# Issuing the FFN input projections in the order of the text

## The chip, the cores and the metric
The kernel runs on one core of a Trainium2 chip. The metric is the device time of one execution in microseconds (us). The engines are TensorE (PE; its weight loads are listed as PEld), VectorE (DVE), ScalarE (ACT), GpSimd (POOL) and SyncE (SP), which here only issues loads.

## The reference, cut to what matters
One step of a two-layer encoder for two request groups, 1024 new frames and 64 frames of a running stream, in float32. Each layer has a mixer and then a gated FFN with a causal convolution of width 3:

```python
def conv_ffn(h, st, w_in, conv_w, conv_b, w_out):     # h: rmsnorm(x), width 1024; D_FF = 2816
    gu = h @ w_in
    g, u = gu[..., :D_FF], gu[..., D_FF:]
    g, new_st = causal_dwconv(g, conv_w, conv_b, st)
    return (jax.nn.gelu(g) * u) @ w_out, new_st
```

The change concerns `h @ w_in` in both layers, and the convolution and gelu beside it.

## The kernel before, in words
Tokens lie along the free dimension (1092 columns with four of padding), channels along the partitions. Float32 accuracy comes from splitting each operand into a rounded part `h` and a remainder `l` and adding three products (`wh x h`, `wl x h`, `wh x l`).

`ffn` (L867) goes through 22 groups for each layer. A group makes two output tiles of 128 channels; a *gate* group makes two tiles of g, and the *up* group after it the two of u that belong to them. A gate and an up group are called a pair here: 11 pairs a layer. For each group `seven` (L396) computes two token blocks of 428 columns with seven products of a half-depth matrix scheme (W, Z1, X1, X2, Z2, X3, Y; 12 instructions of 128x428 each, "wide") and the third block of 236 columns in the plain way (V1 and V0, 24 instructions of 128x236 each, "narrow"): 132 matmul instructions. The results lie in two PSUM tiles of three parts, one bank each: `ta` holds pw, v1, v0, and `tb` holds px, py, pz (L398 to L400). There are two buffers for them, so the next group's tile needs the former one to be read out.

- `held` (L410, tile `cp`) copies a part to SBUF on ScalarE: w, p5, p1, u2. X2 adds onto px after p1 is copied, X3 after u2 is, and Z2 adds onto pz after p5 is.
- `put` (L882 in a gate group, L903 in an up group) adds a part and a copy on VectorE.
- `plain` (L895 gate, L910 up) reads v1 or v0 on VectorE; the one of an up group multiplies by the gelu's result.
- `end` does the rest: for a gate group a multiplication by the norm (L887), the convolution (first tap L248 on ScalarE, two taps L250 on VectorE for each tile), gelu (L890) and another multiplication (L891); for an up group a multiplication (L906) and the store to DRAM (L907, issued by POOL).

The weights of a group are four pairs (h, l) of `ring` tiles: a2, a1, s24, s31. There are eight ring buffers, all in use, so a new pair takes the place of the former group's pair of that name once its last product has read it (V1 for a2, Y for a1, Z2 for s24, X3 for s31). `Ready` (L348) loads two raw tiles through SP (L357; two buffers) and makes one pair with each `step()`: ScalarE rounds (L373), VectorE subtracts (L374), and for a2 and a1 VectorE also makes two combinations in the raw tile (L378, L379; L383, L384).

The order of the work: the framework's planner lists each engine's instructions by priority (the place in the text) and by when it reckons their inputs to be there; it may bring a later instruction forward. It also sets all waits, from which tile an instruction reads or writes. Each engine then runs its list strictly in order. In the text of a middle group the products stand as W, V1, Z1, X1, V0, X2, Y, Z2, X3.

Of the kernel before, what the change touches and what calls it, by code (L numbers as in the profile page):

```python
# [10 lines left out]
AF = mybir.ActivationFunctionType  # L11
# [7 lines left out]
PAD = 4  # L19
S0 = L + PAD  # L20
T = S0 + LS
# [3 lines left out]
SB = 428  # L25
# [5 lines left out]
CONVS = {"ssd": (12, 4), "sc": (8, 3), "lru": (8, 4), "ffn0": (FT, 3), "ffn1": (FT, 3)}  # L31
# [23 lines left out]


def program(nc, tc, a, ctx):
    V, S, G, TE = nc.vector, nc.scalar, nc.gpsimd, nc.tensor
    const = ctx.enter_context(tc.tile_pool(name="const", bufs=1))
    sl = ctx.enter_context(tc.tile_pool(name="sl", bufs=1))  # L60
    wp = ctx.enter_context(tc.tile_pool(name="wp", bufs=1))
# [27 lines left out]
    def wk(cols=T):  # L89
        return slot("wk", 5, F, cols)  # L90
# [8 lines left out]
    def psum():  # L99
        n_of["pm"] = n_of.get("pm", 0) + 1  # L100
        return pm.tile([P, NB, 512], F, tag="pm", name=f"pm{n_of['pm']}")
# [19 lines left out]
    def col(key, i=0, n=1, rows=P):  # L121
        return par[0:rows, AT[key] + i:AT[key] + i + n]
# [33 lines left out]
    def step():  # L156
        if between:
            try:
                next(between[0])
            except StopIteration:  # L160
                between.pop(0)
# [77 lines left out]
        G.memset(cb[:, 0:PAD], 0.0)  # L239
        G.tensor_copy(cb[:, PAD + S0 - n:PAD + S0], col(kind + "_h", i * n, n))  # L240

    def conv(cb, kind, i, out):
        w = CONVS[kind][1]
        history(cb, kind, i)
        G.tensor_copy(keep[kind][:, i, 0], cb[:, PAD + L - w + 1:PAD + L])
        G.tensor_copy(keep[kind][:, i, 1], cb[:, PAD + T - w + 1:PAD + T])
        at = PAD - w + 1
        S.activation(out, cb[:, at:at + T], AF.Identity, bias=col(kind + "_b", i), scale=col(kind + "_w", i * w))  # L248
        for k in range(1, w):
            V.scalar_tensor_tensor(out, cb[:, at + k:at + k + T], col(kind + "_w", i * w + k), out, op0=OP.mult, op1=OP.add)  # L250

    def softplus(x, tmp1, tmp2):

# [15 lines left out]
    class Next:  # L269


        order = range(KT)
        ss = None

        def __init__(self, XR, key, spill=None):
            self.XR, self.key, self.xs, self.spill = XR, key, [], spill
# [18 lines left out]
        def rs(self):  # L295
            return rms(self.ss[0], D, self.ss[1])
# [96 lines left out]
            ready(*last[1])  # L393
            yield

    def seven(ws, X, put, plain, end, nxt, mode="mid", rs=None):  # L396

        ta, tb = psum(), psum()  # L398
        pw, v1, v0 = ta[:, 0, 0:SB], ta[:, 1, 0:RB], ta[:, 2, 0:RB]
        px, py, pz = tb[:, 0, 0:SB], tb[:, 1, 0:SB], tb[:, 2, 0:SB]  # L400

        def mul(ps, w, half, name, start=True, ks=range(HK)):
            for k in ks:
                at = slice((half * HK + k) * P, (half * HK + k + 1) * P)
                wh, wl = ws.w[w][0][:, at], ws.w[w][1][:, at]
                xh, xl = X.part(name, k)
                for i, (wx, x) in enumerate(((wh, xh), (wl, xh), (wh, xl))):
                    TE.matmul(ps, wx, x, start=start and k == 0 and i == 0, stop=k == HK - 1 and i == 2, skip_group_check=True)  # L408

        def held(ps):  # L410
            n = n_of["cp"] = n_of.get("cp", 0) + 1
            t = wp.tile([P, 512], F, tag="wh", bufs=4, name=f"cp{n}")[:, 0:SB]
            S.activation(t, ps, AF.Copy)  # L413
            return t

        def V1():
            mul(v1, "a2", 0, "k0")
            mul(v1, "a2", 1, "k1", False)

        def V0():  # L420
            mul(v0, "a1", 0, "k0")
            mul(v0, "a1", 1, "k1", False)

        def W():
            mul(pw, "a2", 1, "t4")

        def Z1():
            mul(pz, "s31", 1, "t1")

        def Z2():  # L430
            mul(pz, "s24", 1, "b22", False)

        def X1():
            mul(px, "a1", 0, "b11")

        def X2():
            mul(px, "s24", 0, "t2", False)

        def X3():
            mul(px, "s31", 0, "t3", False)  # L440

        def Y():
            mul(py, "a1", 1, "b21")

        step = nxt.step if nxt is not None else lambda: None
        if mode == "mid":
            W()
            V1()
            w = held(pw)
            Z1()  # L450
            plain(1, v1)
            step()
            X1()
            p5 = held(pz)
            V0()
            p1 = held(px)
            X2()
            Y()
            plain(0, v0)
            u2 = held(px)  # L460
            step()
            put(0, 0, py, p1)
            Z2()
        elif mode == "first":
            ws.step()
            Y()
            mul(v1, "a2", 1, "k1")
            mul(v0, "a1", 1, "k1")
            ws.step()
            for k in range(HK):  # L470
                mul(px, "a1", 0, "b11", True, [k])
                mul(pz, "s31", 1, "t1", True, [k])
                mul(pw, "a2", 1, "t4", True, [k])
                mul(v1, "a2", 0, "k0", False, [k])
                mul(v0, "a1", 0, "k0", False, [k])
            p1 = held(px)
            p5 = held(pz)
            w = held(pw)
            rs()
            plain(1, v1)  # L480
            step()
            X2()
            plain(0, v0)
            u2 = held(px)
            put(0, 0, py, p1)
            step()
            Z2()
        else:
            Z1()
            X1()  # L490
            p5 = held(pz)
            W()
            p1 = held(px)
            X2()
            w = held(pw)
            V1()
            u2 = held(px)
            V0()
            plain(1, v1)
            Y()  # L500
            plain(0, v0)
            put(0, 0, py, p1)
            Z2()
        step()
        X3()
        put(0, 1, pz, u2)
        put(1, 0, px, w)
        put(1, 1, px, p5)
        step()
        end(0)  # L510
        end(1)

    def out_weights(w_out, i, n, half):

# [73 lines left out]
    ps = psum()  # L588
# [11 lines left out]
    RS = rms(ss, D)  # L600
# [266 lines left out]
    def ffn(layer, X, done, after):  # L867

        kind = f"ffn{layer}"
        h_d = scratch(f"h_d{layer}", [FT, P, T])  # L870
        two = slice(0, 2 * SB)
        state = {}

        def rs():
            state["rs"] = X.rs()

        def gate(p):
            cbs = [conv_buffer(), conv_buffer()]
            gs = []

            def put(m, b, ps, t):
                V.tensor_add(cbs[m][:, PAD + b * SB:PAD + (b + 1) * SB], ps, t)  # L882

            def end(m):
                RS = state["rs"]
                cb = cbs[m][:, PAD:]
                V.tensor_mul(cb[:, two], cb[:, two], RS[:, two])  # L887
                g = wk()
                conv(cbs[m], kind, 2 * p + m, g)
                S.activation(g, g, AF.Gelu_apprx_tanh)  # L890
                V.tensor_mul(g, g, RS)  # L891
                gs.append(g)

            def plain(m, ps):
                V.tensor_mul(cbs[m][:, PAD + 2 * SB:PAD + T], ps, state["rs"][:, B[2]])  # L895

            return (put, plain, end), gs

        def up(p, gs):
            us = [wk(), wk()]  # L900

            def put(m, b, ps, t):
                V.tensor_add(us[m][:, B[b]], ps, t)  # L903

            def end(m):
                V.tensor_mul(us[m][:, two], us[m][:, two], gs[m][:, two])  # L906
                nc.gpsimd.dma_start(h_d[2 * p + m], us[m])  # L907

            def plain(m, ps):
                V.tensor_mul(us[m][:, B[2]], ps, gs[m][:, B[2]])  # L910

            return put, plain, end

        groups = [(p, u) for p in range(FT // 2) for u in range(2)]

        def ready(g):
            p, u = g
            return Ready(*[("f_in", layer, 2 * (2 * p + m) + u) for m in range(2)])

        ws = X.first  # L920
        gs = None
        for n, (p, u) in enumerate(groups):
            nw = ready(groups[n + 1]) if n + 1 < len(groups) else None
            if u == 0:
                todo, gs = gate(p)
            else:
                todo = up(p, gs)
            seven(ws, X, *todo, nw, "first" if n == 0 else "last" if nw is None else "mid", rs)
            ws = nw

        XR = residual(lambda m: X.spill[m])
        done.XR = XR

        def h_tile(f):
            h = slot("ss", 2) if f == 1 else wk()
            nc.gpsimd.dma_start(h, h_d[f])
            return split(h, x2)

        chunks([2] * (FT // 2), h_tile, a["f_out"][layer], XR, done, after)
        return XR  # L940
# [25 lines left out]
    state = {}  # L966
# [270 lines left out]
```

## Time and profile before

| | us |
|---|---|
| median of 3 runs (2988.62 to 2989.77) | 2989.19 |
| the profiled execution | 2990.91 |
| its span, first to last instruction | 2989.1 |
| TensorE busy | 2759.9 (92%) |
| VectorE busy | 1872.8 (63%) |
| ScalarE busy | 964.1 (32%) |
| products of L408, the changed stage, both layers | 1064.6, idle before them 181.3 |

A row of the profile by lines gives line, engine, operation, output and input tile, shape and count, and the busy time. "Idle before" is the time for which the engine stood in front of such instructions, with what ended it. A matmul's end is modelled, so two that follow each other overlap in the record.

### The profile page before, as it was taken

What the parts mean: (1) busy time and instruction counts of PE and PEld (TensorE: products, weight loads), DVE (VectorE), ACT (ScalarE), POOL (GpSimd) and SP (SyncE); (2) the same over time, 40 slices, a digit from 0 to 9 for tenths busy, and PEclk for the clock granted to TensorE, in tenths of its full rate; (3) what the DMA queues carried; (4) which work ended last, traced back from release to release, by engine and by line L of the source; (5) the groups of instructions that cost most, each with busy time, mean ns of one, the idle gap of its engine ahead of it and who ended that gap; (6) DMA issues with size and microseconds to landing.
All of it is one profiled execution on the core that took longest, in us unless ns stands there. A gap on an engine that the chain in (4) does not pass through costs nothing. (4 is left out here: it accounts for less than half of the span.)

```text
span 2989.1 us, 38889 instructions
## 1 busy us (share of the span) xinstructions
PE 2759.9 (92%) x16132; PEld 2653.2 (89%) x16132; DVE 1872.8 (63%) x2203; ACT 964.1 (32%) x1292; POOL 262.2 (9%) x641
## 2 busy tenths in 40 slices
PE   8999999999988788888999999999888888889998
PEld 8999999999978788787999989989778878879997
DVE  8555655678755555655666768777565565566666
ACT  6323322322432322322221345444332232232113
POOL 1111011110100000000100100121000000001003
PEclk9999999999999899899999999999999999999999
DMA  3223122352411111111522321245111111216221
GB/s 119 85 77 103 48 91 78 105 181 94 138 60 61 48 64 53 58 59 59 200 88 81 113 71 63 75 171 148 51 58 50 67 58 45 72 58 208 88 73 68
DMA packets 81089, 260.16 MB, mean 87 GB/s; under 512 B 9584, under 2 KB 12192, under 8 KB 80912
## 3 DMA queue, kind: packets, MB, share of 16 engines
q0 software_dynamic: 35264, 133.86, 13.4%
q1 hardware_dynamic: 45360, 123.39, 12.9%
q8 instruction: 127, 2.08, 0.3%
q14 instruction: 50, 0.41, 0.0%
q10 hardware_dynamic: 288, 0.42, 0.0%
HBM read 190.36 MB, written 57.21 MB: 83 GB/s over the span
## 5 line engine op out<-in xcount | busy, mean ns | idle before, releaser
L408 PE MATMUL pm<-x,ring 128*128 128x428 f32 (+1 forms) x5808 | 1064.6, 345 | 181.3 <-ACT cp L413 93.5
L408 PEld LDWEIGHTS pm<-x,ring 128*128 128x128 f32 x5808 | 990.0, 203 | 255.0 <-ACT cp L413 111.3
L179 PE MATMUL pm<-x,wh 128*128 128x364 f32 x6048 | 1204.6, 331 | 10.2 <-DVE ring L556 7.5
L179 PEld LDWEIGHTS pm<-x,wh 128*128 128x128 f32 x6048 | 1027.4, 188 | 20.2 <-DVE ring L556 8.8
L179 PE MATMUL pm<-x,wl 128*128 128x364 f32 x3024 | 669.5, 330 | 0.7 <-DVE wl L526 0.6
L179 PEld LDWEIGHTS pm<-x,wl 128*128 128x128 f32 x3024 | 527.4, 189 | 2.0 <-DVE wl L526 1.6
L374 DVE TENSOR_TENSOR ring<-raw,ring 128x1024 fp32r<-128x1024 f32 x176 | 215.0, 1223 | 379.4 <-ACT ring L373 373.3
L556 DVE TENSOR_TENSOR ring<-ring,pm 128x1092 f32<-128x1092 f32 x248 | 319.8, 1290 | 192.1 <-PE pm L179 187.8
L373 ACT ACTIVATE ring<-raw 128x1024 fp32r<-128x1024 f32 x176 | 186.5, 1061 | 736.1 <-PE pm L408 612.2
L525 ACT ACTIVATE wh<-rawo 128x512 fp32r<-128x512 f32 x136 | 84.4, 625 | 355.6 <-PE pm L179 321.4
L143 ACT ACTIVATE wh<-raw 128x512 fp32r<-128x512 f32 x128 | 79.0, 626 | 335.1 <-PE pm L179 334.7
L198 ACT ACTIVATE x<-wk 128x1092 fp32r<-128x1092 f32 x66 | 73.4, 1112 | 236.5 <-PE pm L179 203.4
L250 DVE SCALAR_TENSOR_TENSOR wk<-wk,par,wk 128x1092 f32<-128x1092 f32 x104 | 135.0, 1351 | 10.3 <-ACT wk L248 10.3
L144 DVE TENSOR_TENSOR wl<-raw,wh 128x512 fp32r<-128x512 f32 x128 | 86.7, 683 | 39.9 <-ACT wh L143 39.8
L526 DVE TENSOR_TENSOR wl<-rawo,wh 128x512 fp32r<-128x512 f32 x136 | 90.9, 687 | 29.4 <-ACT wh L525 29.4
L199 DVE TENSOR_TENSOR x<-wk,x 128x1092 fp32r<-128x1092 f32 x66 | 85.3, 1294 | 30.3 <-ACT x L198 30.3
L413 ACT ACTIVATE cp<-pm 128x428 f32<-128x428 f32 x176 | 82.2, 517 | 21.4 <-PE pm L408 21.4
L248 ACT ACTIVATE wk<-wk,par 128x1092 f32<-128x1092 f32 x52 | 65.3, 1296 | 72.4 <-DVE wk L887 64.8
L910 DVE TENSOR_TENSOR wk<-pm,wk 128x236 f32<-128x236 f32 x44 | 17.5, 402 | 99.3 <-PE pm L408 99.3
L240 POOL COPY wk<-par 128x2 f32<-128x2 f32 (+1 forms) x72 | 31.7, 440 | 459.8 <-DVE wk L822 164.0
L907 POOL DMA_DIRECT2D h_d<-wk x44 | 23.4, 533 | 524.7 <-DVE wk L906 523.0
L890 ACT ACTIVATE wk<-wk 128x1092 f32<-128x1092 f32 x44 | 49.0, 1113 | 32.4 <-DVE wk L250 32.2
(278 smaller groups left out, 1997.3 us busy)
## 6 DMA issues: line engine op xcount, KB each, us to landing
raw<-f_in SPq DMA_DIRECT2D x88, 512.0 KB, 3.5
h_d<-wk POOLq DMA_DIRECT2D x44, 546.0 KB, 4.2
wk<-h_d POOLq DMA_DIRECT2D x42, 546.0 KB, 5.0
raw<-ab_in SPq DMA_DIRECT2D x44, 512.0 KB, 3.5
rawo<-f_out SPq DMA_DIRECT2D x88, 256.0 KB, 3.1
ss<-wk POOLq DMA_DIRECT2D x18, 546.0 KB, 5.0
ring<-at_d POOLq DMA_DIRECT2D x16, 546.0 KB, 6.8
rawo<-ab_out SPq DMA_DIRECT2D x32, 256.0 KB, 3.1
```

The source lines that it names most:

```text
L143: S.activation(h, raw, AF.Copy)
L144: V.tensor_sub(l, raw, h.bitcast(F))
L179: TE.matmul(ps[:, b, 0:BL], w, x[:, b * BL:(b + 1) * BL], start=i == 0, stop=i == n - 1)
L199: V.tensor_sub(l, src, h.bitcast(F))
L250: V.scalar_tensor_tensor(out, cb[:, at + k:at + k + T], col(kind + "_w", i * w + k), out, op0=OP.mult, op1=OP.add)
L373: S.activation(h, raw, AF.Copy)
L374: V.tensor_sub(l, raw, h.bitcast(F))
L408: TE.matmul(ps, wx, x, start=start and k == 0 and i == 0, stop=k == HK - 1 and i == 2, skip_group_check=True)
L413: S.activation(t, ps, AF.Copy)
L525: S.activation(h, raw[:, j * 512:(j + 1) * 512], AF.Copy)
L526: V.tensor_sub(l, raw[:, j * 512:(j + 1) * 512], h.bitcast(F))
L556: V.tensor_add(b3(XR[m]), b3(XR[m]), ps[:, :, 0:BL])
```

## The change: what it does
An object around VectorE, ScalarE and TensorE ties, between `in_order(True)` and `in_order(False)`, each instruction of an engine to the one traced before it on this engine, so the planner keeps the order of the text there. POOL and SP are not tied. The text is laid out anew: `end` goes; its work is handed to the next group as two pieces (`pending`), the convolution (or the up group's multiplication and store) and the gelu, and issued after W and after Z1. Reads stand close behind their products, Y ahead of X2, and the weight steps lie later. In the first group the norm's sums (`rs`) follow X2, and `plain` copies without the norm there.

```diff
+    class Ordered:
...
+            def traced(*args, **kwargs):
+                out = call(*args, **kwargs)
+                if order["on"]:
+                    if self.last is not None:
+                        tc.add_manual_dep(out.ins, self.last.name, mybir.DependencyInfo(mybir.DependencyClass.NoSync, mybir.DependencyReason.DATA), reason="in order")
+                    self.last = out.ins
+                return out
...
+    V, S, TE = Ordered(nc.vector), Ordered(nc.scalar), Ordered(nc.tensor)
...
         if mode == "mid":
             W()
+            pending[0]()
             V1()
             w = held(pw)
             Z1()
+            pending[1]()
             plain(1, v1)
-            step()
             X1()
             p5 = held(pz)
             V0()
             p1 = held(px)
-            X2()
+            step()
+            plain(0, v0)
             Y()
-            plain(0, v0)
-            u2 = held(px)
             step()
             put(0, 0, py, p1)
+            X2()
+            u2 = held(px)
             Z2()
         elif mode == "first":
...
             p1 = held(px)
             p5 = held(pz)
             w = held(pw)
+            plain(1, v1)
+            plain(0, v0)
+            X2()
+            put(0, 0, py, p1)
+            u2 = held(px)
             rs()
-            plain(1, v1)
             step()
-            X2()
-            plain(0, v0)
-            u2 = held(px)
-            put(0, 0, py, p1)
             step()
             Z2()
         else:
             Z1()
+            pending[0]()
             X1()
             p5 = held(pz)
             W()
             p1 = held(px)
+            pending[1]()
             X2()
             w = held(pw)
             V1()
...
             put(0, 0, py, p1)
             Z2()
+        put(0, 1, pz, u2)
         step()
         X3()
-        put(0, 1, pz, u2)
         put(1, 0, px, w)
         put(1, 1, px, p5)
         step()
-        end(0)
-        end(1)
...
+            def convs():
                 RS = state["rs"]
+                at = slice(0, T if first else 2 * SB)
+                for cb in cbs:
+                    V.tensor_mul(cb[:, PAD:][:, at], cb[:, PAD:][:, at], RS[:, at])
+                for m, cb in enumerate(cbs):
+                    gs[m] = wk()
+                    conv_first(cb, kind, 2 * p + m, gs[m])
+                for m, cb in enumerate(cbs):
+                    conv_rest(cb, kind, 2 * p + m, gs[m])
+
+            def gelus():
+                for g in gs:
+                    S.activation(g, g, AF.Gelu_apprx_tanh)
+                    V.tensor_mul(g, g, state["rs"])
...
+            def gated():
+                for m in range(2):
+                    V.tensor_mul(us[m][:, two], us[m][:, two], gs[m][:, two])
+                    nc.gpsimd.dma_start(h_d[2 * p + m], us[m])
...
         ws = X.first
-        gs = None
+        gs, pending = None, (nothing, nothing)
+        in_order(True)
         for n, (p, u) in enumerate(groups):
...
+            seven(ws, X, group, pending, nw, "first" if n == 0 else "last" if nw is None else "mid", rs)
+            ws, pending = nw, then
+        pending[0]()
+        in_order(False)
```

## Rows read from the trace of the kernel before

**Rows 1.** The page: busy time, share of the span, instructions of TensorE.
```profile
PE 2759.9 (92%) x16132; PEld 2653.2 (89%) x16132; DVE 1872.8 (63%) x2203; ACT 964.1 (32%) x1292; POOL 262.2 (9%) x641
```
**Rows 2.** Nine pairs, each layer: length; PE, PEld, DVE, ACT, POOL busy (count); granted clock.
```profile
893.57:1404.94 511.37, 436.24 (x2376) 406.32 (x2376) 285.50 (x343) 148.70 (x180) 26.67 (x92) 0.92 0.18 58
2154.30:2661.09 506.79, 433.64 (x2376) 403.84 (x2376) 285.53 (x343) 148.79 (x180) 26.76 (x92) 0.92 0.18 59
```
**Rows 3.** Stretches of wide products (first row) and of V0, layer 0.
```profile
896.50:903.30 6.80, 6.80 (x37) 6.59 (x36) 1.60 (x3) 1.48 (x2) 1.35 (x8) 1.00 0.23 82
893.57:896.30 2.73, 2.73 (x24) 2.73 (x25) 1.23 (x2) 0.00 (x0) 0.00 (x0) 1.00 0.01 5
949.67:953.80 4.13, 4.13 (x24) 4.13 (x25) 1.24 (x2) 0.00 (x0) 1.30 (x3) 0.65 0.00 0
865.99:871.10 5.11, 5.11 (x24) 5.11 (x25) 1.14 (x2) 0.00 (x0) 0.00 (x0) 0.50 0.01 3
```
**Rows 4.** TensorE's largest waits, 893 to 1405 us: total, times, longest.
```profile
PE pm L408 <- ACT cp L413: 46.7, 9, 5.2
PE pm L408 <- DVE wk L895: 17.6, 10, 3.0
PE pm L408 <- DVE wk L910: 5.7, 9, 0.6
```
**Rows 5.** Timeline of TensorE: start, duration; in brackets idle before and releaser.
```profile
865.99 6.53 PE L408 MATMUL pm<-x,ring 128*128 128x236 f32 x27 [5.07 <-DVE wk L910]
...
893.57 10.14 PE L408 MATMUL pm<-x,ring 128*128 128x236 f32 x62 [1.67 <-DVE wk L895]
903.90 7.59 PE L408 MATMUL pm<-x,ring 128*128 128x428 f32 x47 [0.19 <-DVE wk L882]
...
921.63 1.44 PE L408 MATMUL pm<-x,ring 128*128 128x428 f32 x3 [5.17 <-ACT cp L413]
923.70 11.15 PE L408 MATMUL pm<-x,ring 128*128 128x236 f32 x59 [0.63 <-DVE wk L910]
...
949.67 11.80 PE L408 MATMUL pm<-x,ring 128*128 128x236 f32 x62 [2.09 <-DVE wk L895]
```
**Rows 6.** Timeline of the last group, layer 1: put(0,0) and Z2.
```profile
2696.98 0.60 DVE L903 TENSOR_TENSOR wk<-pm,cp 128x428 f32<-128x428 f32 x1 [1.70 <-PE pm L408]
...
2697.64 0.65 PE L408 MATMUL pm<-x,ring 128*128 128x428 f32 x2 [0.77 <-DVE wk L903]
```
**Rows 7.** Timeline of ScalarE: weight roundings, a gelu, three copies.
```profile
901.01 1.06 ACT L373 ACTIVATE ring<-raw 128x1024 fp32r<-128x1024 f32 x1 [7.83 <-PE pm L408]
...
916.62 1.06 ACT L373 ACTIVATE ring<-raw 128x1024 fp32r<-128x1024 f32 x1 [1.43 <-DMA raw<-f_in]
...
919.21 1.11 ACT L890 ACTIVATE wk<-wk 128x1092 f32<-128x1092 f32 x1 [0.15 <-DVE wk L250]
920.23 1.34 ACT L413 ACTIVATE cp<-pm 128x428 f32<-128x428 f32 x3
```
**Rows 8.** Timeline of VectorE around the same two groups.
```profile
902.11 1.22 DVE L374 TENSOR_TENSOR ring<-raw,ring 128x1024 fp32r<-128x1024 f32 x1 [5.15 <-ACT ring L373]
903.25 0.60 DVE L882 TENSOR_TENSOR wk<-pm,cp 128x428 f32<-128x428 f32 x1
903.76 0.68 DVE L383 TENSOR_TENSOR raw<-raw,raw 128x512 f32<-128x512 f32 x1
...
910.41 1.22 DVE L374 TENSOR_TENSOR ring<-raw,ring 128x1024 fp32r<-128x1024 f32 x1
911.55 2.00 DVE L887 TENSOR_TENSOR wk<-wk,ss 128x856 f32<-128x856 f32 x2
914.02 5.16 DVE L250 SCALAR_TENSOR_TENSOR wk<-wk,par,wk 128x1092 f32<-128x1092 f32 x4 [0.47 <-ACT wk L248]
...
920.23 2.50 DVE L891 TENSOR_TENSOR wk<-wk,ss 128x1092 f32<-128x1092 f32 x2
...
923.24 0.40 DVE L910 TENSOR_TENSOR wk<-pm,wk 128x236 f32<-128x236 f32 x1
```

More of the change, by code (lines that the diff above doesn't have):

```diff
@@ L57, in program, with __init__, __getattr__, in_order @@
 def program(nc, tc, a, ctx):
-    V, S, G, TE = nc.vector, nc.scalar, nc.gpsimd, nc.tensor
+    order = {"on": False}
+    class Ordered:
+        def __init__(self, engine):
+            self.engine, self.last = engine, None
+        def __getattr__(self, name):
+            call = getattr(self.engine, name)
+            def traced(*args, **kwargs):
[5 more added lines that the diff above has]
+                return out
+            return traced
+    V, S, TE = Ordered(nc.vector), Ordered(nc.scalar), Ordered(nc.tensor)
+    G = nc.gpsimd
+    def in_order(on):
+        order["on"] = on
+        for e in (V, S, TE):
+            e.last = None
     const = ctx.enter_context(tc.tile_pool(name="const", bufs=1))
@@ L240, in history, with conv_first @@
         G.tensor_copy(cb[:, PAD + S0 - n:PAD + S0], col(kind + "_h", i * n, n))
-    def conv(cb, kind, i, out):
+    def conv_first(cb, kind, i, out):
         w = CONVS[kind][1]
@@ L248, in conv, with conv_rest @@
         S.activation(out, cb[:, at:at + T], AF.Identity, bias=col(kind + "_b", i), scale=col(kind + "_w", i * w))
+    def conv_rest(cb, kind, i, out):
+        w = CONVS[kind][1]
+        at = PAD - w + 1
         for k in range(1, w):
             V.scalar_tensor_tensor(out, cb[:, at + k:at + k + T], col(kind + "_w", i * w + k), out, op0=OP.mult, op1=OP.add)
+    def conv(cb, kind, i, out):
+        conv_first(cb, kind, i, out)
+        conv_rest(cb, kind, i, out)
     def softplus(x, tmp1, tmp2):
@@ L394, in make, with seven @@
             yield
-    def seven(ws, X, put, plain, end, nxt, mode="mid", rs=None):
+    def seven(ws, X, group, pending, nxt, mode="mid", rs=None):
+        put, plain = group
         ta, tb = psum(), psum()
@@ L875, in rs, with gate, plain @@
             state["rs"] = X.rs()
-        def gate(p):
+        def gate(p, first):
             cbs = [conv_buffer(), conv_buffer()]
-            gs = []
+            gs = [None, None]
             def put(m, b, ps, t):
                 V.tensor_add(cbs[m][:, PAD + b * SB:PAD + (b + 1) * SB], ps, t)
-            def end(m):
-                RS = state["rs"]
[L886 to L897, printed above, removed]
+            def plain(m, ps):
+                cb = cbs[m][:, PAD + 2 * SB:PAD + T]
+                if first:
+                    S.activation(cb, ps, AF.Copy)
+                else:
+                    V.tensor_mul(cb, ps, state["rs"][:, B[2]])
+            def convs():
+                RS = state["rs"]
+                at = slice(0, T if first else 2 * SB)
[10 more added lines that the diff above has]
+                    V.tensor_mul(g, g, state["rs"])
+            return (put, plain), (convs, gelus), gs
         def up(p, gs):
@@ L903, in put, with nothing @@
                 V.tensor_add(us[m][:, B[b]], ps, t)
-            def end(m):
-                V.tensor_mul(us[m][:, two], us[m][:, two], gs[m][:, two])
-                nc.gpsimd.dma_start(h_d[2 * p + m], us[m])
             def plain(m, ps):
                 V.tensor_mul(us[m][:, B[2]], ps, gs[m][:, B[2]])
-            return put, plain, end
+            def gated():
+                for m in range(2):
+                    V.tensor_mul(us[m][:, two], us[m][:, two], gs[m][:, two])
+                    nc.gpsimd.dma_start(h_d[2 * p + m], us[m])
+            return (put, plain), (gated, nothing)
+        def nothing():
+            pass
         groups = [(p, u) for p in range(FT // 2) for u in range(2)]
@@ L924, in ffn @@
             if u == 0:
-                todo, gs = gate(p)
+                group, then, gs = gate(p, n == 0)
             else:
-                todo = up(p, gs)
-            seven(ws, X, *todo, nw, "first" if n == 0 else "last" if nw is None else "mid", rs)
-            ws = nw
+                group, then = up(p, gs)
+            seven(ws, X, group, pending, nw, "first" if n == 0 else "last" if nw is None else "mid", rs)
+            ws, pending = nw, then
+        pending[0]()
+        in_order(False)
         XR = residual(lambda m: X.spill[m])
```

## The prediction
> **What bounds the kernel now.** I read the page's busy line first: TensorE is at work for 92% of the span [rows 1], so only its gaps can give time back. Then the changed stage by stretches. From V0 of the second gate group to V0 of the last lie nine pairs of groups, 2376 = 9 x 264 products, in 511.37 us in layer 0 and 506.79 us in layer 1 [rows 2]: 56.6 us a pair. At the full granted clock a wide (428) product comes every 0.194 us (35 in 6.80 us; the 37 counted include two that the edges cut) and a narrow (236) one every 0.112 (24 in 2.73) [rows 3]. A pair without gaps would be 2 x (84 x 0.194 + 48 x 0.112) = 43.4 us, so 13.2 us a pair are lost. TensorE's three large waits make 70.0 us in nine pairs, 7.8 a pair [rows 4]. The rest is short waits and clock: behind a gap of 5.07 us the 24 narrow products of V0 take 5.11 us at a granted clock of 0.50, behind 2.09 us 4.13 at 0.65, behind 1.67 us 2.73 at 1.00 [rows 3, 5].
>
> **What a read makes TensorE wait for.** This decides the forecast. V0 writes the third part of the tile `ta`; plain(1) reads the second part. Nothing of V0 needs plain(1), yet V0 starts at 923.70, 0.06 us after plain(1) (923.24 + 0.40) ends, and in the other group behind L895 at 949.67 [rows 5, 8]. Z2 writes pz; put(0,0) reads py in the same tile `tb`. Z2 starts at 903.90, 0.05 us after put(0,0) (903.25 + 0.60), and so in the last group, 2697.64 after 2696.98 + 0.60 [rows 5, 6, 8]. All nine pairs show it. The reading side is alike: W's copy needs one part only, which was there before 903.90 (W stands ahead of V1), but it runs at 920.23 with those of Z1 and X1 [rows 5, 7]. So I take it that in this program a product waits for every read of any part of its tile that stands before it in the text, and a read for every product before it. In the old text the planner hides part of this by pulling W and two products of V1 ahead of Z2.
>
> The Trainium skill's PSUM — Partial Sum Buffer (PSUM bank collisions raise a hardware error) has two engines collide only in one bank, and different banks run clean. By that rule the thirds, one bank each, need no such wait. The rows disagree on what the program does: its semaphores hold V0 and Z2 back. The rule alone would give the fast rival below.
>
> **The change, step by step.** Each engine now issues in text order, so nothing of the next group can fill a gap. Times below run from W's start, at full clock: W to 2.33, V1 5.0, Z1 7.35, X1 9.7.
>
> *Gate group.* The copy of W and plain(1) come at 5.3 and are done by 5.8; V0 doesn't wait: 9.7 to 12.4. The copies p5 and p1 are over by 11; Y 12.4 to 14.7. Moving a2's weight step behind p1 costs nothing: its load is there about 5.0 us after the former tile's last subtraction (911.63 to 916.62 [rows 7, 8]), that is at 2.5 + 5.0 = 7.5, and ScalarE comes to it at 11.
>
> Then a1's step stands before put(0,0), and X2 behind it. a1's new tiles take the places of those that Y has just read (all eight ring buffers are in use), so: 0.1 to ScalarE, 1.09 to VectorE's L374 (901.01 to 902.11), 1.14 to the next (902.11 to 903.25), 0.68 for L383 and as much for L384, 0.60 for put(0,0), 0.05 to TensorE [rows 7, 8] = **4.3 us** in which TensorE stands. Before, put(0,0) ran between L374 and L383 and W covered it. X2 to 21.3; Z2 now waits for u2's copy: 0.3 + 0.5 + 0.05 = **0.9**; X3 waits for put(0,1), which formerly stood behind it: 0.3 + 0.6 + 0.05 = **0.95**. Group: 21.7 + 6.15 = 27.85.
>
> *Up group.* The same, and V0's wait. VectorE ends the former group's puts and last weight tile at 2.5. From the two multiplications to the end of the convolution are 7.6 us (911.55 to 914.02 + 5.16), so 10.1; the second gelu 1.1, its multiplication 1.25 (2.50 for two), plain(1) 0.40: 12.85 [rows 7, 8] against 9.7, **3.15 us**. What goes is the 5.17 us wait for the copies behind the gelus (p1's ends at 12, ahead of Y's start at 15.5) and the wait for L895. Group: 31.0; the pair 58.9, already 2.3 above 56.6 without any loss of clock.
>
> *Clock.* The pair has gaps of 4.3, 4.3 and 3.15. The rows price a gap of 1.67 us at nothing, of 2.09 at 1.4 and of 5.07 at 2.4 us more for V0 [rows 3, 5]. Bounds for three gaps: 0 and 7.2. I take 1.4 for each, 4.2, the price of the middle row, since the higher one followed the one gap over 5 us. New pair 63.1.
>
> *Ends.* In the first group the norm's three chains move behind X2. VectorE does them and both weight steps before put(0,1), so X3 waits some 6 us; but the old first group too stands until its norm is there. I get the second group's V0 where it was, 0 to 1.5 us later. The last group pays Z1's wait for its own weights (about 2.4), Z2's 0.95 and X3's 0.95: by the same steps 26 us, and the end of the stage 8 us later per layer, estimated from the two groups' sums. POOL's history copies depend on plain() alone and its stores have half a group; SP's loads are issued as before. These cost nothing while they are 3 us early.
>
> *Sum.* 18 pairs x 6.5 = 117, two layers' ends x 9 (8, and 1 for the start) = 18: 135 us over the profiled execution's 2990.9 (its span of 2989.1 and 1.8 around it), 3126; the median of the runs is 1.7 lower: **forecast 3124**.
>
> **Rivals.**
> *A, faster.* If only reads of the same third hold a product, every wait above falls: V0, X2, Z2, X3 have what they need (p1 by 12, X2 at 14.7), VectorE's work for an up group, some 20 us by the durations of rows 8, fits in 21.7, no gap, clock whole: 18 x 13.2 = 238 less, ends 2 x 18 less (the second group's V0 some 8 earlier, the last two groups 10), **2715**. For it: neither V0 nor Z2 uses what it is seen waiting for, so some other cause of the two waits is thinkable. Against it: the same pairs of end and start on every pair of groups [rows 4 to 6, 8]. It decides at the first X2. Chance 0.12.
> *B, much slower.* Gaps come so close that the granted clock stays down for half of the products: at 5.11 against 2.73 us [rows 3] this adds 0.87 to that half: 58.9 + 0.5 x 43.4 x 0.87 = 77.8 a pair, 18 x 21.2 = 382, **3371**. Against it: from X3 through X1 or further 9 to 12 us run without a gap. Chance 0.03.
> *C, it doesn't do what it says* (the planner finds the same order, or the waits for a1's places are shorter so that gains and losses meet): **2989**. Against it: W can't pass Z2 any more. Chance 0.02.
> The forecast case has 0.83. Its own range: no clock loss, each wait a tenth shorter and short ends, 58.4 a pair: 18 x 1.8 + 8 = 40, so 3030; 65.6 a pair, 18 x 9 + 24 = 186, 3175. I widen to **3020 to 3185**. Faster by over 0.2% (about what can be told from no change here) 0.12, within 0.2% 0.02, slower 0.86.
>
> **What would show it.** Right: in nearly every group a gap of about 4.3 us before X2, ended by the put (DVE, behind L384's successor), one of 0.8 to 1.0 before Z2 (the copy) and before X3 (the put), and about 3 us before V0 in up groups only, behind its plain(1); the 5.17 us waits for copies gone; nine pairs in about 568 us; the granted clock below 0.92 there. Wrong: wide products following each other across put(0,0) without a gap (A), or a pair under 58 us, which would mean that a1's step overlaps Y or that the reads are tracked more finely than I read.

## The result and the profile after

The changed kernel takes **3174.51 us** (median of 4 runs, 3169.35 to 3177.55) against 2988.9 for the kernel before: the ratio is 1.0619 [1.06, 1.0637]. The forecast was 3124, within a range of 3020 to 3185. The profiled execution took 3177.55 us, with a span of 3175.7: 186.6 more than the 2989.1 of before. In the traces of after the line of every VectorE, ScalarE and TensorE instruction is that of the helper `traced` (L70, or L72 in some kernels), so they are read by tile: `pm` the PSUM tiles, `cp` ScalarE's copies, `wk` VectorE's results, `ring` weights.

The nine pairs of each layer, from V0 of an up group to V0 nine pairs later (length; PE, PEld, DVE, ACT and POOL busy with counts; granted clock):

```profile
871.71:1457.21 585.50, 453.58 (x2376) 416.05 (x2377) 294.81 (x343) 150.63 (x180) 21.17 (x91) 0.90 0.15 51
2221.09:2810.40 589.31, 457.44 (x2376) 419.85 (x2377) 294.85 (x343) 150.61 (x180) 19.55 (x91) 0.89 0.15 51
```

That is 65.06 and 65.5 us a pair where [rows 2] give 56.6, for the same 2376 products. VectorE and ScalarE do about the same work as before; the time is TensorE's idle time and its clock. Its waits in the first of these stretches (total, times, longest):

```profile
PE pm L70 <- DVE wk L70: 125.4, 46, 4.5
PE pm L70 <- ACT cp L70: 11.1, 18, 0.6
```

136.5 us, 15.2 a pair, against 7.8 for the three waits of [rows 4] and 8.5 with three short ones beside them. The 5.2 us waits for the copies are gone as the change means them to be: what is left of ScalarE's is 0.6. In their place VectorE's results end 46 waits. TensorE's timeline over a whole pair (start, duration, in brackets idle before and what ended it) shows which:

```profile
939.08 6.90 PE L70 MATMUL pm<-x,ring 128*128 128x236 f32 x36 [3.51 <-DVE wk L70]
950.15 4.07 PE L70 MATMUL pm<-x,ring 128*128 128x428 f32 x12 [4.17 <-DVE wk L70]
954.84 2.59 PE L70 MATMUL pm<-x,ring 128*128 128x428 f32 x12 [0.62 <-ACT cp L70]
958.20 17.33 PE L70 MATMUL pm<-x,ring 128*128 128x428 f32 x108 [0.77 <-DVE wk L70]
979.70 3.80 PE L70 MATMUL pm<-x,ring 128*128 128x428 f32 x12 [4.17 <-DVE wk L70]
984.12 2.59 PE L70 MATMUL pm<-x,ring 128*128 128x428 f32 x12 [0.62 <-ACT cp L70]
987.47 12.31 PE L70 MATMUL pm<-x,ring 128*128 128x428 f32 x72 [0.77 <-DVE wk L70]
1003.28 6.87 PE L70 MATMUL pm<-x,ring 128*128 128x236 f32 x36 [3.50 <-DVE wk L70]
```

Read by the text: V0 and Y (36), a gap, X2 (12), a gap, Z2 (12), a gap, then X3, W, V1, Z1, X1 and, in the gate group, V0 and Y without one (108). The four gaps stand where the prediction put them and have the releasers that it named; every middle pair repeats them. A modelled end lies about 0.26 us late (12 wide products are shown as 2.59 but come every 0.194, 2.33), so the true gaps are 4.43, 0.88, 1.03 and 3.76.

The gap before X2, seen from the two engines that it waits for (rows of ScalarE and VectorE):

```profile
975.37 1.06 ACT L70 ACTIVATE ring<-raw 128x1024 fp32r<-128x1024 f32 x1 [2.93 <-PE pm L70]
976.46 1.22 DVE L70 TENSOR_TENSOR ring<-raw,ring 128x1024 fp32r<-128x1024 f32 x1 [0.99 <-ACT ring L70]
977.71 0.69 DVE L70 TENSOR_TENSOR raw<-raw,raw 128x512 f32<-128x512 f32 x1
978.44 0.69 DVE L70 TENSOR_TENSOR raw<-raw 128x512 f32<-128x512 f32 x1
979.05 0.59 DVE L70 TENSOR_TENSOR wk<-pm,cp 128x428 f32<-128x428 f32 x1
```

a1's weight step starts when Y's last product has read the old weights (975.4), runs through rounding, subtraction and two combinations, and only then comes put(0,0) at 979.05, which X2 (979.70) waits for. X2 needs nothing of put(0,0): it adds onto px, and put(0,0) reads py. They share the tile `tb`.

And the clock in stretches of after (columns as in the windows above):

```profile
939.08:943.50 4.42, 4.42 (x25) 4.42 (x26) 2.44 (x3) 0.00 (x0) 0.00 (x0) 0.61 0.02 4
979.70:983.50 3.80, 3.80 (x12) 3.03 (x12) 0.00 (x0) 0.00 (x0) 0.00 (x0) 0.64 0.01 2
```

Behind the 3.51 us gap V0 runs at a granted clock of 0.61, between the levels 1.2 and 2.4 GHz, and takes some 4.4 us instead of the 2.73 of [rows 3]; behind the 4.17 us gap the 12 products of X2 run at 0.64.

### The profile page after: what moved, and what is told of

It reads as the page before. It is cut to its first block, busy times and chain, and to the rows that moved or that the text cites. A ratio compares the mean times of both kernels' runs of the same rounds, so it can differ in the third digit from the quotient of the medians.

```text
span 3175.7 us, 38882 instructions
## 1 busy us (share of the span) xinstructions
PE 2811.9 (89%) x16132; PEld 2687.4 (85%) x16132; DVE 1894.3 (60%) x2199; ACT 971.3 (31%) x1296; POOL 248.5 (8%) x641
## 4 chain that ended last, share of the span: by engine, by line
PE 72%; DVE 15%; ACT 5%; issue 5%; DMA 2%; POOL 1%; DVEq 0%; SPq 0%; ACTq 0%; POOLq 0%
PE pm L70 70%; DVE wk L70 8%; DVE ring L70 3%; PE pa L70 2%; DVE raw L70 2%; ACT ring L70 2%; DVE x L70 1%; ACT wk L70 1%; ACT x L70 1%; ACT cp L70 1%; DMA wk<-h_d 1%; ACT L70 0%; DVE ss L70 0%; DMA ss<-wk 0%; DMA ring<-at_d 0%
## 5 line engine op out<-in xcount | busy, mean ns | idle before, releaser
L70 PE MATMUL pm<-x,ring 128*128 128x428 f32 (+1 forms) x5808 | 1116.4, 356 | 321.5 <-DVE wk L70 285.2
L70 PEld LDWEIGHTS pm<-x,ring 128*128 128x128 f32 x5808 | 1022.9, 210 | 413.7 <-DVE wk L70 242.9
L70 PE MATMUL pm<-x,wh 128*128 128x364 f32 x6144 | 1228.3, 331 | 7.3 <-DVE ring L70 5.4
L70 PEld LDWEIGHTS pm<-x,wh 128*128 128x128 f32 x6144 | 1043.9, 188 | 17.9 <-DVE ring L70 7.1
L70 PE MATMUL pm<-x,wl 128*128 128x364 f32 x3072 | 684.6, 329 | 0.6 <-DVE wl L70 0.6
L70 PEld LDWEIGHTS pm<-x,wl 128*128 128x128 f32 x3072 | 536.1, 188 | 1.3 <-DVE wl L70 0.9
L70 DVE TENSOR_TENSOR ring<-ring,pm 128x1092 f32<-128x1092 f32 (+2 forms) x273 | 332.3, 1222 | 197.0 <-PE pm L70 192.7
L70 DVE TENSOR_TENSOR wk<-pm,cp 128x428 f32<-128x428 f32 x176 | 101.8, 599 | 404.9 <-PE pm L70 404.9
L70 DVE TENSOR_TENSOR ring<-raw,ring 128x1024 fp32r<-128x1024 f32 x176 | 215.1, 1222 | 198.6 <-ACT ring L70 198.3
L70 ACT ACTIVATE ring<-raw 128x1024 fp32r<-128x1024 f32 x176 | 186.0, 1058 | 425.4 <-PE pm L70 407.5
L70 ACT ACTIVATE cp<-pm 128x428 f32<-128x428 f32 x176 | 87.1, 521 | 501.2 <-PE pm L70 497.2
L70 ACT ACTIVATE wh<-rawo 128x512 fp32r<-128x512 f32 x136 | 84.6, 626 | 352.2 <-PE pm L70 315.0
L70 ACT ACTIVATE wh<-raw 128x512 fp32r<-128x512 f32 x128 | 79.1, 626 | 336.2 <-PE pm L70 335.9
L70 ACT ACTIVATE x<-wk 128x1092 fp32r<-128x1092 f32 (+1 forms) x82 | 87.9, 1072 | 238.7 <-PE pm L70 202.8
L70 DVE SCALAR_TENSOR_TENSOR wk<-wk,par,wk 128x1092 f32<-128x1092 f32 x104 | 138.9, 1353 | 13.8 <-ACT wk L70 12.3
L70 DVE TENSOR_TENSOR wk<-wk,ss 128x1092 f32<-128x1092 f32 (+1 forms) x105 | 123.3, 1196 | 0.2
L70 DVE TENSOR_TENSOR x<-wk,x 128x1092 fp32r<-128x1092 f32 (+1 forms) x82 | 101.9, 1243 | 31.2 <-ACT x L70 31.2
L70 DVE TENSOR_TENSOR wk<-pm,ss 128x236 f32<-128x236 f32 (+1 forms) x75 | 61.1, 815 | 84.7 <-PE pm L70 40.8
L70 DVE TENSOR_TENSOR wl<-raw,wh 128x512 fp32r<-128x512 f32 x128 | 86.5, 682 | 40.4 <-ACT wh L70 40.4
L70 DVE TENSOR_TENSOR wl<-rawo,wh 128x512 fp32r<-128x512 f32 x136 | 91.0, 686 | 28.6 <-ACT wh L70 28.6
L70 ACT ACTIVATE wk<-wk 128x1092 f32<-128x1092 f32 x59 | 65.9, 1117 | 82.3 <-DVE wk L70 78.9
L70 DVE TENSOR_TENSOR wk<-pm,wk 128x236 f32<-128x236 f32 (+1 forms) x60 | 38.3, 641 | 86.5 <-PE pm L70 84.6
```

Source lines behind the costliest of these rows:

```text
L70: out = call(*args, **kwargs)
```

## The experiments

The theory under test, **T**: a product waits for every earlier read of its whole PSUM tile, of which the parts are three banks, and the change takes away the planner's means to fill those waits. Rivals: the tie alone costs the time; a1's weight step, or the wait for p1's copy, is what X2 really needs; the loss is the clock's alone. Each time is the median of four runs, each ratio against the kernel before with its interval.

**One bank to a tile, all else as changed.** The pool of three-part tiles is replaced by six one-bank buffers for the length of the loop.

```diff
-        ta, tb = psum(), psum()
-        pw, v1, v0 = ta[:, 0, 0:SB], ta[:, 1, 0:RB], ta[:, 2, 0:RB]
-        px, py, pz = tb[:, 0, 0:SB], tb[:, 1, 0:SB], tb[:, 2, 0:SB]
+        pw, v1, v0 = bank(SB), bank(RB), bank(RB)
+        px, py, pz = bank(SB), bank(SB), bank(SB)
```

> The changed kernel with the six parts (pw, v1, v0, px, py, pz) as six PSUM tiles of one bank each, in place of two tiles of three parts; text, order and arithmetic as in the changed kernel. Theory T (a product waits for the reads of other parts of its tile that stand before it in the text): the gaps before X2 (4.17 us), Z2 (0.62), X3 (0.77) and V0 (3.5) go, a middle pair of groups falls from 65 us to 44 to 46, the time to 2715 to 2760. Rival R1 (issuing in order makes the gaps: what V0 and X2 truly need, such as p1's copy behind the gelus, is late): a pair stays above 58, the time above 3060. Rival R2 (TensorE can't stream a whole group at the full granted clock): a pair of 50 to 56, 2830 to 2940.

Measured: 2729.36 us, 0.912 [0.9107, 0.9134]. TensorE's timeline has one stretch of 427 products over more than three groups, without any gap, and the clock stays whole:

```profile
929.77 70.49 PE L72 MATMUL pb<-x,ring 128*128 128x236 f32 x427
```
```profile
900.00:1250.00 350.00, 350.00 (x2135) 341.06 (x2134) 263.12 (x307) 137.49 (x163) 16.95 (x80) 1.00 0.23 76
```

350 us for 2135 products are 43.3 for the 264 of a pair: the dense 43.4 that the prediction worked out from [rows 3]. No data, no order and no work differ from the changed kernel, only which reads a product is made to wait for (and that six banks come free one by one). All four waits go at once, so T holds, and neither the weight step nor a copy was needed in time. The Trainium skill's PSUM — Partial Sum Buffer (PSUM bank collisions raise a hardware error) has engines collide within a bank and run clean in different ones; this run agrees with it, TensorE writing one bank at 100% while VectorE and ScalarE read others.

**put(0,0) ahead of a1's step, tiles as changed.**

```diff
             Y()
             plain(0, v0)
-            step()
             put(0, 0, py, p1)
+            step()
             X2()
```

> The changed kernel with put(0,0) ahead of a1's weight step, nothing else. T: the gap before X2 falls from 4.17 us to about 0.77 (one VectorE add behind Y), 3.4 us in each of 40 middle groups, 136 us, and 1 to 2 us of clock in each, 40 to 70 us: 2975 to 3000. R1 (X2 waits for p1's copy): no change, 3165 to 3180.

Measured: 2963.15 us, 0.9905 [0.9888, 0.9921], 12 below the lower end of what was expected. The gap before X2 falls from 4.17 to 0.69, the others keep their size:

```profile
981.16 6.88 PE L70 MATMUL pm<-x,ring 128*128 128x236 f32 x36 [3.50 <-DVE wk L70]
988.74 2.62 PE L70 MATMUL pm<-x,ring 128*128 128x428 f32 x12 [0.69 <-DVE wk L70]
991.97 2.59 PE L70 MATMUL pm<-x,ring 128*128 128x428 f32 x12 [0.62 <-ACT cp L70]
```

So X2 needs a1's new weights not at all, only VectorE's read that stood behind them. Of the 211 us that this saves over the changed kernel the gaps explain 3.48 for each of 40 middle groups, 139. The other 72 go with the clock: X2 now takes 2.62, where it took 3.70 to 4.65 in the trace of after, 4.26 on average (1.6 for each of 40 groups), and the granted clock from 900 to 1250 us is 0.97 instead of 0.90.

**The gaps filled with idle products.** 18 wide products of weights and data that are there anyway, into a spare bank, before X2, and 14 before V0 of up groups; their results are not read.

```diff
+            if pending[1] is not nothing:
+                spin(14)
             V0()
...
+            spin(18)
             X2()
```

> The changed kernel with idle work for TensorE in the two large gaps of the middle groups: 18 wide products into a spare bank between Y and X2, 14 before V0 in up groups; they are read by nobody and fit into the gaps. If the excess over my sum is the granted clock (T with a larger price for the clock): the clock stays at 1.00 in the middle groups, a pair falls from 65.0 to about 59, 18 x 6 = 108 us, 3060 to 3075. If the clock loss is 4.2 a pair as I took it: 3095 to 3105. If the clock costs nothing and the gaps themselves are longer: 3170 or above.

Measured: 3070.94 us, 1.0263 [1.0248, 1.0278]. Here the waits are all still there, and only TensorE's idle time in them is used up:

```profile
936.36 5.28 PE L70 MATMUL pm<-x,ring 128*128 128x236 f32 x36 [0.80 <-DVE wk L70]
941.47 3.65 PE L70 MATMUL pa<-x,ring 128*128 128x428 f32 x18
945.82 2.61 PE L70 MATMUL pm<-x,ring 128*128 128x428 f32 x12 [0.69 <-DVE wk L70]
...
996.27 3.91 PE L70 MATMUL pm<-x,ring 128*128 128x236 f32 x29 [0.79 <-DVE wk L70]
```

From V0 to V0 a pair takes 59.9 us (936.36 to 996.27), against 65.06; the granted clock from 900 to 1250 us is 1.00, where it was 0.90. So the clock costs the changed kernel 5.2 us a pair and, the ends with it, 104 us (3174.5 less 3070.9). That is the price against the full clock, and not the clock's share of the 186 us lost, since the kernel before pays for its clock too (0.92 in [rows 2]): of its 13.2 us a pair some 3 are left for the clock when its waits are taken off (an estimate: 8.5 as shown and 0.26 more for each of seven). By that estimate some 2 of the 8.5 us by which a pair grew (56.6 to 65.06) are the clock's, and the rest are gaps. No run filled the gaps of the kernel before.

**Only `ta` split, `tb` whole.** This separates V0's wait from the others.

```diff
+        pw, v1, v0 = bank(SB), bank(RB), bank(RB)
+        tb = psum()
```

> The changed kernel with only ta split into three one-bank tiles (pw, v1, v0); tb stays one tile of three parts. T: V0's gap of 3.5 us in up groups goes with its clock loss, the gaps before X2, Z2 and X3 stay at 4.17, 0.62 and 0.77: a pair of 58 to 60 in place of 65, 18 x 5 to 7 us, 3050 to 3090. If the waits hang together (one moves into the other): above 3130.

Measured: 3110.61 us, 1.0395 [1.0377, 1.0412], 20 above the upper end. The waits did as expected: V0's 3.50 is gone, the three on `tb` stay (X2's in up groups is 4.45 to 4.47, the others as shown).

```profile
970.84 4.65 PE L72 MATMUL pm<-x,ring 128*128 128x428 f32 x12 [4.17 <-DVE wk L72]
976.10 4.42 PE L72 MATMUL pm<-x,ring 128*128 128x428 f32 x12 [0.62 <-ACT cp L72]
981.28 2.62 PE L72 MATMUL pm<-x,ring 128*128 128x428 f32 x12 [0.77 <-DVE wk L72]
```

The size missed by the clock. V0's own loss is gone (its 24 products take 2.84), but X2's 12 products now take 4.6 us on average instead of 4.26, and Z2's take 4.3 to 4.45 in ten of the 40 middle groups, where the trace of after has five such. The granted clock from 900 to 1250 us is 0.87, in the same stretch of after 0.90. So the wait came back and next to nothing of the clock: 20 waits of 3.76 would be 75 us, 64 came back.

**The middle text in another order, three-part tiles kept.** V1 and V0 follow each other behind the gelus, the reads of `ta` behind both, where Y covers them, and put(0,0) stands ahead of both weight steps. The order of the text in short:

```diff
-  W, pending0, V1, w, Z1, pending1, plain1, X1, p5, V0, p1, step, plain0, Y, step, put00, X2, u2, Z2
+  W, pending0, Z1, X1, p5, p1, pending1, V1, V0, w, plain1, plain0, Y, put00, step, X2, u2, step, Z2
```

> The changed kernel with the middle text laid out for waits between parts, tiles as they were: W, Z1, X1, copies p5 and p1, gelus, V1, V0, then the reads w, plain(1), plain(0), Y, put(0,0), a2's step, X2, u2, a1's step, Z2. T: V0 waits for no read, X2 only for one add (about 0.7), Z2 and X3 as before (0.62, 0.77): a pair near 49 us, 2850 to 2890. If V0's or X2's gap had another cause (operands, the gelus): above 2930.

Measured: 2887.51 us, 0.9652 [0.9638, 0.9667]: tied text order and three-part tiles, and 3.5% below the kernel before, once the order is laid out by what the program's waits are.

```profile
933.73 17.39 PE L70 MATMUL pm<-x,ring 128*128 128x428 f32 x108 [1.57 <-DVE wk L70]
951.82 2.59 PE L70 MATMUL pm<-x,ring 128*128 128x428 f32 x12 [0.70 <-DVE wk L70]
955.03 2.61 PE L70 MATMUL pm<-x,ring 128*128 128x428 f32 x12 [0.62 <-ACT cp L70]
959.20 17.42 PE L70 MATMUL pm<-x,ring 128*128 128x428 f32 x108 [1.56 <-DVE wk L70]
```

A group takes 25.5 us (933.73 to 959.20), with three gaps of 0.6 to 1.6, and the clock is 1.00. The pair is 2 us above the 49 expected: X3's gap is 1.57 where 0.77 was taken over from after.

**The new text without the tie.** `in_order(True)` is left out.

> The new text with the planner free to reorder (in_order never switched on). T: the waits before X2, Z2 and X3 stand in the text and stay, but the planner may bring W and V1 of the next group forward into them: between 2990 and 3120. If the tied order alone is what costs: back to 2985 to 2995 or below.

Measured: 2962.46 us, 0.9897 [0.988, 0.9914], 28 below the lower end that T gave. I had expected the planner to find less: it fills the waits before X2, Z2 and X3, and what stays is V0's, 5.47 in up groups and 2.60 here in gate groups, where the changed kernel had none:

```profile
947.94 19.67 PE L70 MATMUL pm<-x,ring 128*128 128x236 f32 x109 [2.60 <-DVE wk L70]
978.46 21.80 PE L70 MATMUL pm<-x,ring 128*128 128x236 f32 x117 [5.47 <-DVE wk L70]
```

So on this text the tie costs 212 us with the three-part tiles, by taking from TensorE what it would do in these waits.

**The text before with the tie.** `Ordered` and `in_order` around the loop of before, nothing else.

> The kernel before with in_order switched on around the same loop: the old text, tied. It tells the cost of the tie from that of the new text. T: Z2 waits in every group for put(0,0) behind a1's step (about 4.2 us) with nothing to fill it, V0 in up groups for the plain read behind the gelus (about 3); X2 and X3 don't wait for a put. A pair of 58 to 61, 3030 to 3080: between before and the changed kernel. If the tie costs nothing with the old text: 2985 to 2995. If the tie is all of the loss: 3165 or more.

Measured: 3253.27 us, 1.0871 [1.0855, 1.0888], 173 above the upper end. I had left out that the old `end` goes through convolution and gelu tile by tile, so in order plain(1) comes far later; the wait before V0 is 8.82 in up groups, and 4.88 before Z2 in every group:

```profile
943.25 9.46 PE L70 MATMUL pm<-x,ring 128*128 128x236 f32 x48 [8.82 <-DVE wk L70]
957.58 23.34 PE L70 MATMUL pm<-x,ring 128*128 128x428 f32 x132 [4.88 <-DVE wk L70]
```

The time lies where the expectation put a tie that is all of the loss, and with three-part tiles it is: alone the tie costs 264 us, and the new text alone saves 26. What the runs with one-bank tiles add is how it costs: through the waits between parts, and on the old text through one true need besides.

**The kernel before with one-bank tiles** (the planner free, the first diff above applied to it).

> The kernel before (old text, planner free) with the six parts as six one-bank tiles. T: the planner's order was laid out around the waits between parts; without them V0 and Z2 are free, and a pair falls from 56.6 us well below 50: 2730 to 2860. If the tied order is needed for the gain of the six-tile kernel: above 2900.

Measured: 2785.08 us, 0.9306 [0.9292, 0.9319]. The waits of [rows 4] for L895 and L910 are gone, and of the copy's 5.2 us 1.8 is left, once a pair, which takes 45.5 us (910.14 to 955.65):

```profile
910.14 43.67 PE L421 MATMUL pb<-x,ring 128*128 128x428 f32 x264 [1.83 <-ACT cp L426]
955.65 45.24 PE L421 MATMUL pb<-x,ring 128*128 128x428 f32 x264 [1.84 <-ACT cp L426]
```

**The same, tied.**

> The old text tied, with six one-bank tiles. T: the waits between parts go (8.8 us before V0 in up groups, 4.9 us before Z2 in all), but a true wait stays: ScalarE takes p1's copy behind the old text's convolution and gelus, so X2 stands some 7 us in up groups: 2870 to 2960. If the old text's loss when tied is waits between parts alone: 2720 to 2760.

Measured: 2951.78 us, 0.9869 [0.9852, 0.9885]. One gap a pair is left, and it is a true need: X2 adds onto px, which p1's copy must have read, and in the old text that copy stands behind the gelus.

```profile
979.72 20.58 PE L72 MATMUL pb<-x,ring 128*128 128x428 f32 x108 [7.74 <-ACT cp L72]
```

This is the wait of 5.17 in [rows 5] that the new text is laid out to avoid, and it does, with either kind of tile.

**The new text, one-bank tiles, no tie.**

> The new text with six one-bank tiles and the planner free (the six-tile kernel without in_order). T: with no waits between parts both orders keep TensorE fed: 2720 to 2790. If the tie itself is worth something once the tiles are split: 2760 or more, slower than the tied one by more than 20 us.

Measured: 2719.51 us (2716.64 to 2720.3), 0.909 [0.9076, 0.9103]: 9% below the kernel before, at the lower end of what was expected, and with the next version, which can't be told from it, the fastest.

**Tied, one-bank tiles, the last group in a middle group's order.** `"first" if n == 0 else "mid"`.

> The six-tile kernel with the last group's text like a middle group's, so that W covers the wait for s31: about 1.9 us less per layer where TensorE waits for it, 2722 to 2730; if the operands of the next stage come later for it, 2730 to 2740.

Measured: 2721.32 us, 0.9096 [0.9083, 0.911], 8 us below the tied version with the last group's own text and as fast as the free one. The last group's own text has Z1 ahead of its own weights; its two waits there, of 0.9 to 1.0 us in each layer, are gone, and the wait at the head of the next stage falls from 3.3 to 1.4 in layer 0 and from 2.6 to 1.4 in layer 1. That the 10 us between tied and free lie in that group is not shown by this: the changed stage takes 489.0 us here in layer 0 (first to last product) and 484.3 in the free kernel, so the two are equally fast in all but not stage by stage.

Together, medians in us (the kernel before measured 2988.9 to 2993.5 beside them, so a few us between two cells say nothing):

| | three-part tiles, planner free | three-part, tied | one-bank, free | one-bank, tied |
|---|---|---|---|---|
| text before | 2988.9 | 3253.3 | 2785.1 | 2951.8 |
| new text | 2962.5 | 3174.5 | 2719.5 | 2729.4 |

## Why the prediction was right

- **What a read holds.** The step on which all hung, read off V0's and Z2's starts in [rows 5, 6, 8], is shown: taking tiles apart, and that alone, removes the waits (all six parts: all of them; `ta` only: V0's only). Rival A's price of 2715 was right for a program whose reads hold one part; the one-bank tiles gave 2729. It is not the program that the change makes. The reading side holds too, and the rows of the prediction showed it less well, since W's copy stood behind other work there. In a gate group X3's end lets ScalarE round (first row of each pair below) and W follows X3. With three-part tiles W's copy comes 5.3 us later, behind W and V1; with one-bank tiles 2.6 us later, behind W alone (ScalarE, after and then one-bank):

```profile
960.65 1.06 ACT L70 ACTIVATE ring<-raw 128x1024 fp32r<-128x1024 f32 x1 [2.32 <-PE pm L70]
965.92 0.53 ACT L70 ACTIVATE cp<-pm 128x428 f32<-128x428 f32 x1 [4.21 <-PE pm L70]
```
```profile
961.95 1.06 ACT L72 ACTIVATE ring<-raw 128x1024 fp32r<-128x1024 f32 x1 [1.27 <-PE pb L72]
964.50 0.53 ACT L72 ACTIVATE cp<-pb 128x428 f32<-128x428 f32 x1 [1.49 <-PE pb L72]
```

- **X2's gap.** Forecast 4.3, measured 4.43 (4.17 shown), by the steps summed there: 0.1 to the rounding, 1.09 from the rounding's start to VectorE's, 1.25 to the first combination, 0.73, 0.61 and 0.65 to X2.
- **Z2's and X3's.** Forecast 0.9 and 0.95, measured 0.88 and 1.03. The 0.3 us from a product's end to the reader had no row in the prediction; after shows 0.30 and 0.36.
- **V0's, in up groups only.** Forecast 3.15, measured 3.76. From the former group's two multiplications to the end of the convolution VectorE takes 7.9 us instead of 7.6, and the last gelu, multiplication and plain(1) follow a little further apart. VectorE's timeline of after has the chain:

```profile
992.28 2.00 DVE L70 TENSOR_TENSOR wk<-wk,ss 128x856 f32<-128x856 f32 x2
994.76 5.41 DVE L70 SCALAR_TENSOR_TENSOR wk<-wk,par,wk 128x1092 f32<-128x1092 f32 x4 [0.47 <-ACT wk L70]
1000.08 2.56 DVE L70 TENSOR_TENSOR wk<-wk,ss 128x1092 f32<-128x1092 f32 x2
1002.73 0.41 DVE L70 TENSOR_TENSOR wk<-pm,wk 128x236 f32<-128x236 f32 x1
```

- **The gaps' sum.** 2 x (4.43 + 0.88 + 1.03) + 3.76 = 16.4 a pair, forecast 15.45: 1.0 short.
- **The clock.** Forecast 4.2 a pair; 65.06 less 43.4 and 16.4 leaves 5.2 (5.7 in layer 1), and the run with the gaps filled gives the same 5.2. The middle row's price of 1.4 for a gap was too low for gaps of 3.5 to 4.2: X2's 12 products lost 1.1 to 2.0, V0 with Y behind it 1.6 (6.90 against 5.28). The prediction chose that row because the dearer one "followed the one gap over 5 us". That is a misreading: [rows 4, 5] have a gap of 5.2 us in every pair, and behind the one before 921.63 the trace of before shows the clock down as well:

```profile
921.60:928.00 6.40, 5.74 (x27) 5.14 (x28) 2.64 (x4) 0.00 (x0) 0.00 (x0) 0.58 0.00 0
```

- **The ends.** Forecast 18 us for both layers. The nine pairs of the two layers lost 74.1 and 82.5 (585.50 - 511.37 and 589.31 - 506.79), 156.7 against the forecast's 117; so 186.6 - 156.7 = 30 lie outside them. In layer 0 V0 of the first up group starts at 871.71, 5.7 us later than the 865.99 of [rows 5], where 0 to 1.5 were forecast. X3's wait there is 6.40, as forecast (some 6), but the long wait of the old first group, which I had let cancel it, is 3.67 only. That is 2.7 of the 5.7; the rest was not taken apart. Layer 1 starts 5.9 us later in the same way. The end of the stage is as forecast: 8.1 and 9.1 us later, where 8 stood. TensorE's timeline, after and then before:

```profile
852.42 14.75 PE L70 MATMUL pm<-x,ring 128*128 128x428 f32 x72 [6.40 <-DVE wk L70]
```
```profile
844.51 16.41 PE L408 MATMUL pm<-x,ring 128*128 128x428 f32 x84 [3.67 <-DVE wk L895]
```

What was to show the forecast right did so (a pair above 58 us, the granted clock below 0.92, the copies' waits gone); the nine pairs took 585.5 and 589.3 us instead of "about 568". The sum of 135 was 52 short of the 186.6: 40 by gaps and clock in the pairs, 12 by the ends. The terms were mis-sized all in one direction, since the clock was priced by the middle row and V0's chain by its shortest; the upper end of the own range, 65.6 a pair and 24 for the ends, 3175, is what came. The prediction gives no working for 65.6, so that it lies so near the measured 65.06 and 65.5 is in part luck.

## What to carry to other kernels

Before an order is tied, find out which reads the program's waits really hold a product back for: if one tile spans several banks, a read of any part may hold all of them, and the gaps in which a free planner would have moved other work become idle time. Take the tile apart first (here 204 us on the kernel before, 445 on the changed one); then the new order is worth 66 us more, and the tie is worth nothing (10 us slower). And price a row of gaps with the clock's loss behind each, not by the gaps alone.

## What the runs showed of the hardware

- TensorE given work whose results nobody reads makes the kernel faster: 50 idle products added to each pair (18 before each X2, 14 before V0 in the up group) took 104 us off; the waits they stand in were not shortened, only the granted clock rose, from 0.90 to 1.00.
- Three gaps of 0.6 to 1.6 us in each group of 25.5 cost no clock (1.00 in the reordered kernel), while gaps of 3.5 to 4.2 put it at 0.61 to 0.64 for the products behind them. The Trainium skill's TensorE: Matmul & The Clock Gate (A second HAM failure mode: psum-queue depth-cycling) tells of a kernel whose clock goes up and down through short idles between groups of products; these rows agree for the longer gaps, and not for the shorter.
- A wait removed need not give back its clock: with V0's gap gone V0 ran at full clock, but X2's products behind their gaps of 4.2 to 4.5 took 4.6 us on average instead of 4.26, Z2's behind a gap of only 0.62 took 4.3 to 4.45 in ten groups of 40 instead of five, and the granted clock from 900 to 1250 us was 0.87 instead of 0.90. What in the spacing of the gaps does this was not tried and stays open.
